# The rounded key and query blocks transposed by a plain fp32r product instead of an fp32 transpose

## The chip, the cores and the metric

The program runs on one core of a Trainium2 chip, in one launch. The metric is the device time of one execution in microseconds; the time given for a kernel is the median of its runs.

## The reference, cut to what matters

One layer of a hybrid decoder on 1024 tokens of width 1024, in float32. Each token is normalised and projected into nine groups of 256 columns; pooling, a short gated convolution, a Conformer convolution and a differential attention work on them; one output projection adds the result to the input, and a SwiGLU block of inner width 2816 follows. The part that the change touches is the attention's scores: four heads, each with two maps of 32 columns.

```python
def diff_attention(q, k, v, q_norm_g, k_norm_g, lam, lam_init, subln_g, rel_bias):
    q = rms_norm(q, q_norm_g)
    k = rms_norm(k, k_norm_g)
    ...
        sc = jnp.einsum('bqhmd,bkhmd->bhmqk', qblk, k).astype(jnp.float32) * scale + bias
        sc = jnp.where(dist >= 0, sc, NEG_INF)
        p = jax.nn.softmax(sc, axis=-1)
        a = p[:, :, 0] - lam * p[:, :, 1]
        return jnp.einsum('bhqk,bkhd->bqhd', a.astype(v.dtype), v)
```

The products have to be nearly as exact as float32.

## The kernel before, in words

Every large product is made of three products in fp32r, a rounded float32 that TensorE takes: an operand is split into a rounded part `hi` and a rounded rest `lo`, and hi·hi, hi·lo and lo·hi are summed in PSUM (`mm3`, L138 to L140; the same three as L604 to L606 where they are handed out one at a time). The tokens stand in eight tiles of 128, worked on in four pairs p of 256 tokens.

The stages in order: norms, input projections and convolutions up to 165 us; then the projections of keys, queries and values by tokens (`proj_tok`, L473, the products `mm` L138 to L140 of 256 columns) up to 246 us; then the attention, 16 units u (`unit`, L657), four heads for each of the four pairs, up to about 405 us; then the second norm and the SwiGLU block to the end.

`stack_T` (L498) prepares keys and queries for the scores. For a token tile of 128 and a group g of two heads it makes the tile `kst` (128 partitions, 4 x 128 columns, type fp32r): ScalarE rounds the values into it (`hi`, L505), VectorE or GpSimd writes the rounded rest (`lo`, L506), each twice, in an order in which one product of 128 rows gives hi·hi + hi·lo + lo·hi + lo·lo. Then TensorE transposes the four 128x128 blocks of `kst` into a PSUM tile (L510), and ScalarE copies them to `KT` or `QT` as fp32r (L513). There are 32 such groups of four transposes: 16 for keys and 4 for queries in the stage of the projections (PSUM tile `t`, 80 transposes), 12 for queries within the attention (PSUM tile `tp`, 48). Before, the block is read as float32 (`bitcast(F)`), and the other operand is `ident`, a 128x128 identity in float32, made by GpSimd at the start.

A unit computes scores (L673, PSUM `sc`), VectorE takes the row minimum of the negated scores (L680, L681), ScalarE the exponential (L684), VectorE joins the two maps (L687, L688, tile `pt`); TensorE transposes `pt` (L699), ScalarE rounds it to `at` (L703), VectorE writes the rest (L704), and TensorE multiplies with the values (L708, PSUM `av`: of 256 columns, and of 128 in the last block of each pair). Other products are handed out between these steps to fill TensorE: parts of the output projection (L604 to L606, `fm`, with `sp` and later `mh`, `ml`), norms (L190), later the first products of the SwiGLU block.

The order of the instructions on each engine is not written by hand. A scheduler sets it when the program is built, by priorities and by its own estimate of how long each instruction takes; the tables at the top (`FQ`, `FL`, `FA`, `FB`, `FC`) say how many filling products are handed out at each place. The hardware then runs each engine's list in that order. So an instruction to which the scheduler gives another length can change the order of others.

Of the kernel before, what the change touches and what calls it, by code (L numbers as in the profile page):

```python
# [11 lines left out]
F = mybir.dt.float32  # L12
R = mybir.dt.float32r
# [6 lines left out]
P = 128  # L20
# [46 lines left out]
def tile_hybrid(ctx, tc, x, norm1_g, w_in, pool_w, pool_scale, sconv_w, conf_w, conf_b, ln_g, ln_b,  # L67
                q_g, k_g, lq1, lk1, lq2, lk2, subln_g, w_out, norm2_g, w_gate, w_up, w_down,
                rel_bias, onehot, maskrow, cntinv, out):
    nc = tc.nc  # L70
    V, A, G, T = nc.vector, nc.scalar, nc.gpsimd, nc.tensor
# [11 lines left out]
    def pool(name, bufs=1, side="left", **kw):  # L83
        return tc.tile_pool(name=name, bufs=bufs, side=side, reuse_waits="tile", **kw)

    const = ctx.enter_context(pool("const"))
# [13 lines left out]
    def ps_mm():  # L100
        return psm.tile([P, 512], F, name="mm", tag="mm")
# [3 lines left out]

    ident = const.tile([P, P], F, name="ident")
    make_identity(nc, ident)
    mhalf = const.tile([P, 16], F, name="mhalf")
    G.memset(mhalf, -0.5)
    G.memset(padl, 0.0)  # L110
# [117 lines left out]
    def chunk_mm(W, ps, h, o, c0, n):  # L228
        for kt in range(8):
            ins = mm3(ps[:, o:o + n], (W[0][:, kt], W[1][:, kt]), (hT[h][0][:, kt, c0:c0 + n], hT[h][1][:, kt, c0:c0 + n]),  # L230
                      kt == 0, kt == 7)
        return ins
# [9 lines left out]
    for p in range(4):  # L242
# [18 lines left out]
        for j in range(2):  # L261
            if p % 2 == 0:
                ps0[j][h] = ps_mm()
            ins = chunk_mm(W0[j], ps0[j][h], h, c0, c0, 256)
# [108 lines left out]
    ps = ps_mm()  # L373
# [84 lines left out]
    for q in range(2):  # L458
        ps = ps_mm()
# [38 lines left out]
    def stack_T(kn, dst, isq, ps_new, nm, g, fill=None, p=None):  # L498
        for i in range(2):
            st = misc.tile([P, 4, 128], R, name="kst", tag="mi") if isq else spp.tile([P, 4, 128], R, name="kst", tag="sp")  # L500
            sv = st.rearrange("p m (a b d) -> p m a b d", a=2, b=2)
            src = kn[:, i, g * P:(g + 1) * P].rearrange("p (m d) -> p m d", d=32).unsqueeze(2).broadcast_to([P, 4, 2, 32])
            hi = sv[:, :, 0, :, :] if isq else sv[:, :, :, 0, :]
            lo = sv[:, :, 1, :, :] if isq else sv[:, :, :, 1, :]
            A.copy(hi, src)  # L505
            (G if isq and X3[2 * PO.index(p) + g] else V).tensor_tensor(lo, src, hi.bitcast(F), op=ALU.subtract)  # L506
            for m in range(0, 4, nm):
                ps = ps_new()
                for a in range(nm):
                    ins = T.transpose(ps[:, a * P:(a + 1) * P], st[:, m + a, :].bitcast(F), ident)  # L510
                if fill:
                    fill(ins)
                A.copy(dst[:, m:m + nm, i * P:(i + 1) * P], ps[:, 0:nm * P].rearrange("p (a b) -> p a b", a=nm))  # L513
# [3 lines left out]
    def prep_q(p, g, ps_new, nm, fill=None):  # L517
        QT[p, g] = qtp.tile([P, 4, 256], R, name="QT", tag="QT")
        stack_T(qn[p], QT[p, g], True, ps_new, nm, g, fill, p)

    def use_k(p, ps):
        ln_pair(p)
        kn = qn[p]
        qk_norm(ps, kn.rearrange("p a b -> p (a b)"))
        for g in range(2):
            stack_T(kn, KT[g][:, :, p * 256:(p + 1) * 256], False, ps_t2, 4, g)
# [657 lines left out]
```

## Time and profile before

| what | us |
|---|---|
| median of 3 runs | 1082.94 (1082.12 to 1084.14) |
| the profiled execution | 1081.06 |
| its span, first to last instruction | 1079.3 |
| PE busy in the span | 1051.2 (97%) |
| DVE busy | 732.8 (68%) |
| ACT busy | 438.9 (41%) |
| POOL busy | 222.5 (21%) |
| granted TensorE clock, mean over the span | 1.000 |

PE is TensorE's products, PEld its weight loads (each product loads its stationary operand first, beside the product before it), DVE is VectorE, ACT ScalarE, POOL GpSimd, SP the queue that issues transfers. A product's duration in a row runs from its start to the end of its modelled pipeline, so neighbours overlap; what a product costs TensorE is the distance between starts. Shares of busy time are averages over stages with different limits.

### The profile page before, as it was taken

To read this page: it belongs to the slowest core of one execution; us is meant where nothing else is said; L and a number is where in the kernel's file an instruction comes from. 1 tells how busy PE (TensorE), PEld (TensorE's weight loads), DVE (VectorE), ACT (ScalarE), POOL (GpSimd) and SP (SyncE) were. 2 spreads that over 40 slices of the span, in tenths; PEclk is the share of its full clock that TensorE was granted. 3 is DMA by queue.
4 is the path that set the end of the run, shared out by engine and by line. 5 is a ranking of instruction groups with operands and counts; after the bars stand their busy time and mean duration, and the time that the engine had idled before them with its cause. 6 is when DMAs were issued, how large, how long until landed. Compare 5 with 4: busy or idle time off the path is not lost.

```text
span 1079.3 us, 13508 instructions
## 1 busy us (share of the span) xinstructions
PE 1051.2 (97%) x5203; PEld 875.7 (81%) x5203; DVE 732.8 (68%) x1127; ACT 438.9 (41%) x710; POOL 222.5 (21%) x202
## 2 busy tenths in 40 slices
PE   7999999998989999899999999999999999999998
PEld 7878879996778876788878888888888888888886
DVE  5599984657899966888677675556656567555541
ACT  5512124545786766432332333333333244333320
POOL 5137114655676653000000000000000000000000
PEclk9999999999999999999999999999999999999999
DMA  8131210111021121014576663233223268766721
GB/s 216 49 98 40 59 39 20 40 40 40 30 71 47 50 81 37 14 54 154 210 280 244 250 208 108 73 112 127 88 79 127 106 228 296 246 195 214 231 101 39
DMA packets 89664, 128.04 MB, mean 119 GB/s; under 512 B 17112, under 2 KB 57600, under 8 KB 87040
## 3 DMA queue, kind: packets, MB, share of 16 engines
q1 hardware_dynamic: 89600, 127.18, 36.0%
q8 instruction: 41, 0.67, 0.3%
q14 instruction: 23, 0.19, 0.1%
HBM read 94.13 MB, written 33.04 MB: 118 GB/s over the span
## 4 chain that ended last, share of the span: by engine, by line
PE 81%; DVE 9%; DMA 5%; ACT 2%; issue 1%; POOL 1%; SPq 0%; ACTq 0%; DVEq 0%; POOLq 0%
PE sb L140 10%; PE sb L138 10%; PE sb L139 10%; PE mm L138 6%; PE mm L139 6%; PE mm L140 6%; PE dx L140 3%; PE dx L138 3%; PE dx L139 3%; PE dy L140 3%; PE dy L138 3%; PE dy L139 3%; DMA wd<-in_w_down_dram 2%; DMA dT<-wd 2%; PE fm L606 1%; PE fm L604 1%
## 5 line engine op out<-in xcount | busy, mean ns | idle before, releaser
L138 PE MATMUL sb<-T,rhi 128*128 128x512 f32 x320 | 125.6, 392 | 0.0
L140 PE MATMUL sb<-T,rlo 128*128 128x512 f32 x320 | 125.5, 393 | 0.0
L139 PE MATMUL sb<-T,rhi 128*128 128x512 f32 x320 | 125.5, 392 | 0.0
L911 DVE TENSOR_TENSOR dq<-ds,dq 128x2048 fp32r<-128x2048 f32 x35 | 80.1, 2291 | 60.3 <-ACT dq L910 60.1
L910 ACT CAST dq<-ds 128x2048 fp32r<-128x2048 f32 x35 | 66.8, 1910 | 105.5 <-PE dy L140 39.6
L134 POOL TENSOR_TENSOR wlo<-st,whi 128x1024 fp32r<-128x1024 f32 (+2 forms) x30 | 73.4, 2449 | 113.0 <-ACT whi L120 101.9
L138 PE MATMUL mm<-hT,whi 128*128 128x512 f32 (+1 forms) x224 | 81.0, 373 | 2.4 <-ACT whi L120 1.9
L139 PE MATMUL mm<-hT,whi 128*128 128x512 f32 (+1 forms) x224 | 82.8, 373 | 0.3 <-DVE hT L200 0.2
L140 PE MATMUL mm<-hT,wlo 128*128 128x512 f32 (+1 forms) x224 | 82.1, 370 | 0.0
L317 DVE SCALAR_TENSOR_TENSOR t<-u,cw,t 128x1023 f32<-128x1023 f32 (+28 forms) x58 | 71.4, 1267 | 0.7
L138 PEld LDWEIGHTS sb<-T,rhi 128*128 128x128 f32 x320 | 60.1, 188 | 13.7 <-DVE tp L1030 0.4
L139 PEld LDWEIGHTS sb<-T,rhi 128*128 128x128 f32 x320 | 60.1, 188 | 13.5
L140 PEld LDWEIGHTS sb<-T,rlo 128*128 128x128 f32 x320 | 60.1, 188 | 13.5
L910 ACT CAST rhi<-st 128x1024 fp32r<-128x1024 f32 x28 | 29.4, 1051 | 85.2 <-PE sb L139 46.5
L140 PE MATMUL dx<-dq 128*128 128x512 f32 x160 | 62.4, 390 | 0.0
L139 PE MATMUL dx<-dq 128*128 128x512 f32 x160 | 62.3, 389 | 0.0
L138 PE MATMUL dx<-dq 128*128 128x512 f32 x160 | 61.9, 390 | 0.0
L684 ACT ACTIVATE pt<-sc,mx 128x128 f32<-128x128 f32 (+7 forms) x64 | 47.6, 747 | 18.2 <-DVE mx L681 18.2
L138 PE MATMUL mm<-whi,hT 128*128 128x256 f32 x192 | 54.8, 288 | 0.0
L139 PE MATMUL mm<-wlo,hT 128*128 128x256 f32 x192 | 54.5, 285 | 0.0
L140 PE MATMUL mm<-whi,hT 128*128 128x256 f32 x192 | 54.4, 284 | 0.0
L120 ACT CAST whi<-st 128x1024 fp32r<-128x1024 f32 x28 | 29.4, 1050 | 58.8 <-PE mm L139 52.8
(342 smaller groups left out, 2683.6 us busy)
## 6 DMA issues: line engine op xcount, KB each, us to landing
ds<-dL SPq DMA_DIRECT2D x35, 512.0 KB, 4.0
wd<-in_w_down_dram SPq DMA_DIRECT2D x10, 1024.0 KB, 5.0
dT<-wd SPq DMA_DIRECT2D x10, 1024.0 KB, 4.0
dL<-afs SPq DMA_DIRECT2D x10, 1024.0 KB, 4.4
ds<-dT SPq DMA_DIRECT2D x20, 512.0 KB, 5.4
st<-in_w_in_dram SPq DMA_DIRECT2D x18, 512.0 KB, 3.7
st<-in_w_gate_dram SPq DMA_DIRECT2D x15, 512.0 KB, 4.0
st<-in_w_up_dram SPq DMA_DIRECT2D x15, 512.0 KB, 3.6
```

Source lines behind the costliest of these rows:

```text
L120: A.copy(dst, src)
L134: G.tensor_tensor(lo[:, nv:], st[:, nv:], hi[:, nv:].bitcast(F), op=ALU.subtract)
L138: T.matmul(ps, lhsT=L[0], rhs=Rr[0], start=first, stop=False, skip_group_check=more)
L139: T.matmul(ps, lhsT=L[0], rhs=Rr[1], start=False, stop=False, skip_group_check=more)
L140: return T.matmul(ps, lhsT=L[1], rhs=Rr[0], start=False, stop=last, skip_group_check=more)
L317: V.scalar_tensor_tensor((z if s == 30 else acc)[:, s:], u[:, :S - s], w[:, 30 - s:31 - s], acc[:, s:], op0=ALU.mult, op1=ALU.add)
L604: yield lambda: T.matmul(ps, lhsT=L[0], rhs=Rr[0], start=first, stop=False)
L606: yield lambda: T.matmul(ps, lhsT=L[1], rhs=Rr[0], start=False, stop=last)
L684: A.activation(pts[m][:, 0:w], sc[:, 0:w], AF.Exp, bias=mx, scale=-1.0, accum_out=lt[:, h, m, i:i + 1])
L910: A.copy(hi, src)
L911: (eng or V).tensor_tensor(lo, src, hi.bitcast(F), op=ALU.subtract)
```

## The change

A second identity, `identr`, of type fp32r is made by a ScalarE copy of `ident`. L510 becomes a plain product: the fp32r block of `kst` is the stationary operand as it is, `identr` the moving one. The values are already rounded, so the product with ones and zeros gives the same numbers. Nothing else in the source changes; lines after L107 stand two lines further down, so L510 is L512 in the changed kernel, L673 is L675, and so on.

```diff
     ident = const.tile([P, P], F, name="ident")
     make_identity(nc, ident)
+    identr = const.tile([P, P], R, name="identr")
+    nc.scalar.copy(identr, ident)
...
-                    ins = T.transpose(ps[:, a * P:(a + 1) * P], st[:, m + a, :].bitcast(F), ident)
+                    ins = T.matmul(ps[:, a * P:(a + 1) * P], lhsT=st[:, m + a, :], rhs=identr, start=True, stop=True)
```

The scheduler sets another order. On TensorE, where the last query projection gives way to the values (about 221 us), `mm` are the projections' products, and before the order is:

```order
L138 MATMUL mm<-whi,hT_101 128x256
L139 MATMUL mm<-wlo,hT_101 128x256
L140 MATMUL mm<-whi,hT_102 128x256
L510 MATMUL t_1868<-ident,kst 128x128 x4
L510 MATMUL t_1877<-ident,kst 128x128 x4
L138 MATMUL mm<-whi,hT_101 128x256
L139 MATMUL mm<-wlo,hT_101 128x256
L140 MATMUL mm<-whi,hT_102 128x256
```

Here the two groups of four transposes follow each other. At the same place the changed kernel has on TensorE:

```order
L141 MATMUL mm<-wlo,hT_103 128x256
L142 MATMUL mm<-whi,hT_104 128x256
L140 MATMUL mm<-whi,hT_103 128x256 x2
L141 MATMUL mm<-wlo,hT_103 128x256
L142 MATMUL mm<-whi,hT_104 128x256
L512 MATMUL t_1870<-identr,kst 128x128 x4
L140 MATMUL mm<-whi,hT_103 128x256
L512 MATMUL t_1879<-identr,kst 128x128 x4
L141 MATMUL mm<-wlo,hT_103 128x256
L142 MATMUL mm<-whi,hT_104 128x256
```

The two groups of key transposes stand some six products later, with one product between them. The other moves in this stage are of one to three products.

On TensorE near the end of the attention (381 us before) `sc` is the last pair of score products of the last unit, `tp<-ident,pt` the transposes of the unit before it. Before:

```order
L673 MATMUL sc<-KT_1365,QT 128x512 x2
L708 MATMUL av<-at,VV_1375 128x256 x2
L751 MATMUL tp<-ident,qn_1379 128x128 x4
L708 MATMUL av<-at,VV_1375 128x256 x2
L699 MATMUL tp<-ident,pt 128x128 x4
L604 MATMUL fm<-whi,mh 128x512
L605 MATMUL fm<-wlo,mh 128x512
L606 MATMUL fm<-whi,ml 128x512
L604 MATMUL fm<-whi,mh 128x512
L605 MATMUL fm<-wlo,mh 128x512
L606 MATMUL fm<-whi,ml 128x512
L699 MATMUL tp<-ident,pt 128x128 x4
```

Here the score products come first. The changed kernel has on TensorE:

```order
L753 MATMUL tp<-ident,qn_1381 128x128 x4
L710 MATMUL av<-at,VV_1377 128x256 x4
L701 MATMUL tp<-ident,pt 128x128 x4
L606 MATMUL fm<-whi,mh 128x512
L607 MATMUL fm<-wlo,mh 128x512
L608 MATMUL fm<-whi,ml 128x512
L606 MATMUL fm<-whi,mh 128x512
L607 MATMUL fm<-wlo,mh 128x512
L608 MATMUL fm<-whi,ml 128x512
L701 MATMUL tp<-ident,pt 128x128 x4
L675 MATMUL sc<-KT_1367,QT 128x512 x2
```

The last score products have moved behind two groups of transposes, the first six `mh`/`ml` products of the output projection and products with the values.

On VectorE over the same time the `pt` of 1024 columns is the last unit's, `fmx` and the ISA rows lead up to it, and `at` belongs to the unit before. Before:

```order
L704 TENSOR_TENSOR at<-tp,at 128x512
L680 TENSOR_REDUCE fmx<-sc 128x1
L686 RECIPROCAL cf<-lt 128x1
L759 SCALAR_TENSOR_TENSOR ml<-tp,subg,mh 128x512
L681 ISA sc,mx<-sc,tb,fmx 128x256
L681 ISA mx 128x1
L704 TENSOR_TENSOR at<-tp,at 128x512
L687 SCALAR_TENSOR_TENSOR cf<-lt,nlam,cf 128x1
L736 SCALAR_TENSOR_TENSOR l_4524<-lt 128x8
L688 SCALAR_TENSOR_TENSOR pt<-pt,cf 128x1024
L704 TENSOR_TENSOR at<-tp,at 128x512
L704 TENSOR_TENSOR at<-tp,at 128x384
```

Here one `at` stands between the last `fmx` and the `pt`, and two stand behind it. The changed kernel has on VectorE:

```order
L706 TENSOR_TENSOR at<-tp,at 128x512
L682 TENSOR_REDUCE fmx<-sc 128x1
L706 TENSOR_TENSOR at<-tp,at 128x512
L683 ISA sc,mx<-sc,tb,fmx 128x256
L683 ISA mx 128x1
L689 SCALAR_TENSOR_TENSOR cf<-lt,nlam,cf 128x1
L738 SCALAR_TENSOR_TENSOR l_4526<-lt 128x8
L690 SCALAR_TENSOR_TENSOR pt<-pt,cf 128x1024
L706 TENSOR_TENSOR at<-tp,at 128x384
```

Now two `at` of 512 stand on either side of the last `fmx`, and only the last `at`, of 384 columns, stands behind the `pt`. On SP the order is unchanged; on ACT the table load and the one new CAST stand first, and some thirty instructions of the attention change places with neighbours.

## Rows read from the trace of the kernel before

**Rows 1.** Stretches: us, busy time and count by engine, clock, DMA

```profile
core 0: us, PE busy (x) PEld busy (x) DVE busy (x) ACT busy (x) POOL busy (x), PEclk, DMA share, GB/s
182.00:246.00 64.00, 64.00 (x549) 64.00 (x548) 34.17 (x62) 31.77 (x63) 39.72 (x31) 1.00 0.11 34
246.00:340.00 94.00, 85.42 (x471) 69.36 (x470) 85.43 (x252) 67.27 (x178) 62.15 (x63) 1.00 0.16 51
340.00:380.00 40.00, 40.00 (x236) 34.45 (x235) 37.26 (x78) 28.62 (x54) 25.97 (x28) 1.00 0.13 41
380.00:470.00 90.00, 82.88 (x412) 65.18 (x411) 68.62 (x130) 48.95 (x87) 23.70 (x20) 1.00 0.15 47
```

**Rows 2.** L510 alone: duration in ns min/median/max, first and last start

```profile
L510 PEld LDWEIGHTS t<-ident,kst x80: 138/140/144, 182.8 to 244.5; 128*128 128x128 f32 x80
L510 PE MATMUL t<-ident,kst x80: 270/273/277, 182.9 to 244.6; 128*128 128x128 f32 x80
...
L510 PE MATMUL tp<-ident,kst x48: 270/273/328, 263.4 to 361.2; 128*128 128x128 f32 x48
```

**Rows 3.** Timeline of PE: start us, duration us, line, tiles, shape, count

```profile
182.80 0.28 PE L140 MATMUL mm<-whi,hT 128*128 128x256 f32 x1
182.92 1.03 PE L510 MATMUL t<-ident,kst 128*128 128x128 f32 x8
183.71 0.36 PE L138 MATMUL mm<-whi,hT 128*128 128x256 f32 x1
183.91 0.27 PE L139 MATMUL mm<-wlo,hT 128*128 128x256 f32 x1
```

**Rows 4.** Timeline of PE around one fp32r product of 128 columns

```profile
289.53 0.22 PE L708 MATMUL av<-at,VV 128*128 128x128 f32 x1
289.59 0.44 PE L605 MATMUL fm<-wlo,sp 128*128 128x512 f32 x1
289.87 0.39 PE L606 MATMUL fm<-whi,sp 128*128 128x512 f32 x1
290.10 0.40 PE L604 MATMUL fm<-whi,sp 128*128 128x512 f32 x1
```

**Rows 5.** Timeline of PEld at the same place: each product's weight load

```profile
289.53 0.19 PEld L605 LDWEIGHTS fm<-wlo,sp 128*128 128x128 f32 x1
289.64 0.19 PEld L606 LDWEIGHTS fm<-whi,sp 128*128 128x128 f32 x1
289.87 0.19 PEld L604 LDWEIGHTS fm<-whi,sp 128*128 128x128 f32 x1
```

**Rows 6.** Groups by shape, 246 to 470 us: count, busy us, mean ns

```profile
L708 PE MATMUL av<-at,VV 128*128 128x128 f32 x32 | 7.1, 222 | 0.0
```

**Rows 7.** Waits of PE, 246 to 470 us: total us, times, longest

```profile
PE av L708 <- DVE at L704: 3.1, 3, 1.3
...
PE tp L699 <- DVE pt L688: 1.9, 4, 0.8
```

**Rows 8.** Timeline of PE and DVE, end of the attention, waits in brackets

```profile
381.12 0.61 PE L673 MATMUL sc<-KT,QT 128*128 128x512 f32 x2
...
382.96 0.50 PE L708 MATMUL av<-at,VV 128*128 128x256 f32 x2 [0.56 <-DVE at L704]
...
390.12 0.50 PE L708 MATMUL av<-at,VV 128*128 128x256 f32 x2 [1.28 <-DVE at L704]
...
392.58 0.62 PE L699 MATMUL tp<-ident,pt 128*128 128x128 f32 x4
...
387.19 2.28 DVE L688 SCALAR_TENSOR_TENSOR pt<-pt,cf 128x1024 f32<-128x1024 f32 x1
```

**Rows 9.** Timeline of ACT and POOL at the start

```profile
0.72 1.28 ACT L170 ACT_TABLE_LOAD   x1 [0.72 <-PEq L1172]
4.53 0.63 ACT L170 ACTIVATE xn<-xt 128x512 f32<-128x512 f32 x1 [2.53 <-DMA xt<-in_x_dram]
...
1.10 0.29 POOL masks.py:199 TENSOR_SCALAR_AFFINE_SELECT ident<-ident 128x128 f32<-128x128 f32 x1
```

## The prediction

> **What bounds the kernel now.** I read the stretches first, then the line of the transposes, then the timeline around one group of them, then the waits. The stretches [rows 1] say where TensorE sets the pace: from 182 to 246 us it is busy for all of the 64.00 us, and from 340 to 380 us for all of 40.00. Around the second it stands still at times: 94.00 - 85.42 = 8.6 us between 246 and 340, and 90.00 - 82.88 = 7.1 us between 380 and 470. The changed line [rows 2] has 80 of its 128 transposes, from 182.8 to 244.5 us, in the stretch without idle time, and 48, from 263.3 to 361.1, in the attention. In the first stretch every nanosecond of the new product counts, in either direction. In the attention VectorE is busy for 85.43 of the 94 us [rows 1] and TensorE waits for it as often as for anything [rows 7]; there a nanosecond counts in part.
>
> **What a transpose costs now.** In the timeline [rows 3] eight transposes start at 182.92, and the second product after them starts at 183.91. The usual step between products of 256 columns is 0.12 (182.80 to 182.92), and one of the two products after the group has that step. So the eight cost 183.91 - 182.92 - 0.12 = 0.87 us, 109 ns each. (The first product behind them starts only 0.03 after the last transpose, but its own successor comes 0.20 after it, so the distance must be read over both.) 128 of them are 14.0 us.
>
> **What the new product costs.** No row shows four such products in succession, but 32 products of the same kind are there: fp32r, a 128x128 stationary block and 128 moving columns, in the multiplication with the values [rows 6]. One row of them lasts 222 ns against 273 of the transpose [rows 2], so its stream through the array is shorter by about 50 ns. That is what "single-pass" promises, and it is not what TensorE pays. In [rows 4] such a product starts at 289.53, the next at 289.59, but that one's successor comes at 289.87, 0.28 later where the step between products of 512 columns is 0.23 (289.87 to 290.10). Over both, the product of 128 columns costs 289.87 - 289.53 - 0.23 = 0.11 us. The reason stands in the weight loads [rows 5]: the load for the next product starts at 289.53 and the one after it at 289.64. A weight load of an fp32r block holds the loading path for 0.11 us; beside a product of 256 or 512 columns that is hidden, beside one of 128 it is not. The old transpose is the opposite case: its load is the shorter one (140 ns in its row [rows 2], 190 in [rows 5]), and its product the longer.
>
> So I take 0.11 us for each new product, that is 110 to 111 ns, against 109. The direct term is 128 x (+1 to +2 ns) = +0.1 to +0.3 us; I take +0.1. The bounds: the least is the step of 0.06 to the next start (289.53 to 289.59), if loads of successive short products could overlap after all: 128 x (60 - 109) = -6.3 us, of which 80 x 49 ns = 3.9 us lie in the stretch without idle time. The most is the step of the next wider shape, 0.12: 128 x 11 = +1.4 us. The nearest row is the same shape itself, so the value is near the middle and not at the lower end.
>
> The Trainium skill, TensorE: Matmul & The Clock Gate, section "LDWEIGHTS", gives a load as the number of columns over 1.2 GHz, which for 128 is 107 ns; the trace agrees with 0.11 between loads [rows 5]. The same page, section "Back-to-back issue gap", measures about 81 ns for each product in a stream of loads and products of 128 columns; by it the sum would be an estimated 128 x (81 - 109 ns) = -3.6 us. No row here has such a stream, and the lone products speak for 0.11.
>
> **The added copy.** ScalarE writes `identr` once. It loads its table from 0.72 to 2.00 and then stands idle until the first input lands at 4.53; `ident` is ready at 1.39 [rows 9]. A copy of 128 columns has 2.5 us of room and needs a fraction of it. Cost 0; if that cover were gone, its own length, which cannot be over the 0.63 of the four times wider ACTIVATE behind it [rows 9].
>
> **What moves in the first stretch.** Transposes move by one to seven products of 0.12 us among products that need none of them. TensorE has no wait here, and its queue stays as long. The keys that come up to 0.8 us later are read by scores only after 246 us. Cost 0.
>
> **What moves in the attention.** This is the larger unknown. From about 300 us the scheduler's order changes, and at the end it changes most. Before, the last score products start at 381.12 and the last `pt` ends at 387.19 + 2.28 = 389.47, a chain of 8.35 us; its first transposes start at 392.58, so it has 3.1 us to spare [rows 8]. In the new order the scores come later and between them and those transposes stand, by my count of the rows, 18 products of 512, 10 of 256, two of 128 and seven transposes: 18 x 0.23 + 10 x 0.12 + 2 x 0.11 + 7 x 0.109 = 6.3 us. So that slack is gone and the chain, if it still took 8.35, would be 2.05 late. But the chain was long because VectorE had other work in its queue; in the new order one `at` fewer stands behind the long `pt`, and the two waits for `at` behind `pt` of 0.56 and 1.28 us [rows 8] have more products in front of them. I expect 2.05 against 0.56 + 1.28 = 1.84, so +0.2, and nothing at the smaller moves, since the same work stands in the same engines. Bounds: no wait left between 380 and 470 us beyond what the norms ask, -2.5 (the 1.84 and some 0.7 of other small ones out of 7.1); or one more wait of 2.05 in the stretch from 340 to 380 that now has none, with both old ones kept, about +4.
>
> **Sum.** +0.1 and 0 and 0 and +0.2 make +0.3 on the profiled execution of 1081.06 us (its span of 1079.3 and 1.8 around it): 1081.4. That execution lies 1.9 below the median of the runs, 1082.94, and I carry the same difference over: 1083.2 us.
>
> **Rivals.**
> 1. The shorter stream shows: successive short products cost 60 ns. For it speaks the duration of 222 against 273, against it the load at 289.64. It gives 3.9 us before 246 us and half of 48 x 49 ns = 2.4 us in the attention, -5.1 us: 1077.9. Chance 0.11.
> 2. Loads and products overlap in part in a row of four or eight, at about 85 ns, half way between 60 and 111: 80 x 24 ns = 1.9 and half of 48 x 24 ns, -2.5 us: 1080.5. The measured stream that the Trainium skill gives (above) lies here. Chance 0.07.
> 3. The later scores decide. The place is the transposes of `pt` in the last two units; the price is 2.05 us each, less the 1.84 that goes, so +2.3, and with the direct term at up to +1.4 some +3: 1085.9. It decides from the point where the chain from scores to `pt` takes more than 6.3 + 1.84 us. For it speaks that VectorE is busy 37.26 of the 40 us from 340 to 380 [rows 1]; against it that the scores were early before. Chance 0.20.
> 4. The new order saves the two waits and adds none, -2.5 us: 1080.5. Chance 0.07.
>
> That the change does nothing at all to the time is the forecast itself: a product with another limit for the same price.
>
> **How the numbers follow.** 0.2% is 2.2 us, about what a measurement of this kernel can tell from no change. The forecast, between -1.5 and +2 us, has 0.55. Faster by over 0.2%: rival 1 with 0.11, most of rivals 2 and 4 with 0.11, together 0.22. Slower: most of rival 3 and the top of the forecast, 0.20. Within: 0.58. The range for 8 in 10 leaves out the lower half of rival 1 and the upper part of rival 3: 1078.3 to 1086.6. The forecast's own range is 1081.4 to 1085.2.
>
> **What would show it.** Right: in the profile after, the products of L512 last about 220 ns, but eight of them still take 0.87 to 0.90 us by the same reading over two successors, with their weight loads 0.11 apart and 190 ns long; the stretch from 182 us ends within 0.4 us of 246. Wrong, by rival 1: starts 0.06 apart throughout and the projections over 3 us earlier. For the order: waits of TensorE for `pt` L690 or `at` L706 after 340 us, against 3.1 and 1.9 us now [rows 7]. My prediction fails at its main step if the eight take under 0.7 us.

## The result and the profile after

| what | us |
|---|---|
| before, median of 6 runs beside it | 1083.1 (1080.13 to 1085.98) |
| after, median of 6 runs | 1088.2 (1087.79 to 1091.12) |
| ratio | 1.0054, 95% interval 1.0033 to 1.0074 |
| the profiled execution after | 1089.98, its span 1088.2 |

The change makes the kernel 5.1 us slower by the two medians. The ratio in the table, from which later sections work, is not their quotient (1.0047); it would make 5.8 us. The forecast was 1083.2, with a range up to 1086.6. The two profiled executions are 8.9 us apart (1081.06 and 1089.98), so some of what follows belongs to one execution and not to the change.

**The new product.** The changed line in the profile after, as [rows 2] (min/median/max in ns):

```profile
L512 PEld LDWEIGHTS t<-identr,kst x80: 187/192/193, 181.6 to 243.6; 128*128 128x128 f32 x80
L512 PE MATMUL t<-identr,kst x80: 218/273/278, 181.7 to 243.7; 128*128 128x128 f32 x80
L512 PE MATMUL tp<-identr,kst x48: 221/276/330, 262.3 to 360.6; 128*128 128x128 f32 x48
```

And the timeline of PE around the first eight, as [rows 3]:

```profile
181.57 0.28 PE L142 MATMUL mm<-whi,hT 128*128 128x256 f32 x1
181.69 1.00 PE L512 MATMUL t<-identr,kst 128*128 128x128 f32 x8
182.53 0.33 PE L140 MATMUL mm<-whi,hT 128*128 128x256 f32 x1
182.70 0.28 PE L141 MATMUL mm<-wlo,hT 128*128 128x256 f32 x1
```

By the same reading as in the prediction, over two successors, the eight cost 182.70 - 181.69 - 0.12 = 0.89 us, 111 ns each, against 0.87 before. The duration in the row is not the 222 ns of the lone product [rows 6]: in a row of them it is 273. I read the difference as the wait for the product's own weight load; the rows do not show it apart. The loads of the eight, in the timeline of PEld, from the first to the one behind them:

```profile
181.57 0.98 PEld L512 LDWEIGHTS t<-identr,kst 128*128 128x128 f32 x8
182.47 0.19 PEld L140 LDWEIGHTS mm<-whi,hT 128*128 128x128 f32 x1
```

(182.47 - 181.57) / 8 = 0.11 us from load to load.

**Where the time went.** The stretches, as [rows 1]:

```profile
182.00:246.00 64.00, 64.00 (x544) 63.91 (x543) 32.44 (x63) 32.46 (x64) 39.56 (x31) 1.00 0.11 34
246.00:340.00 94.00, 84.86 (x465) 68.78 (x464) 85.41 (x252) 66.98 (x178) 61.12 (x63) 1.00 0.16 51
340.00:380.00 40.00, 39.20 (x226) 33.21 (x225) 34.40 (x72) 26.53 (x52) 23.58 (x28) 1.00 0.12 41
380.00:470.00 90.00, 81.13 (x404) 63.11 (x403) 67.81 (x129) 49.95 (x89) 24.49 (x20) 1.00 0.16 47
```

The stretch from 340 to 380 us has lost its full PE (40.00 to 39.20), and VectorE does 2.9 us less there (37.26 to 34.40). To place the loss I compared the start of the same product of TensorE in both traces; the numbers are after minus before, in us, at the product that stood at the given time before:

| trace | 25 | 244 | 340 | 440 | 570 | 620 |
|---|---|---|---|---|---|---|
| after | -1.2 | -1.0 | -0.2 | +3.8 | +3.0 | +8.9 |

The start is 1.2 us earlier in this execution. The 80 products before 246 us cost +0.2. Between 293 and 306 us +0.8 is lost, then between 340 and 440 +4.0. At the product that stood at 380 the shift is already +2.4, up from -0.5 at 366. But from 360 to 415 many products have changed places, so that the shift of one product holds its own move too. Counted instead by the work that TensorE had started (each product at its usual step of 0.23, 0.12 or 0.11 us for 512, 256 or 128 columns, so an estimate), the shift goes from -0.1 at 366 to +2.4 at 380 and +3.2 at 382, back to +1.8 at 392, where the two old waits lay, and up again to +4.0 at 430. From 540 to 570 us 0.8 is regained, and behind 574 us comes another +5.9. The waits of PE from 246 to 470 us, as [rows 7], with two more rows of before ahead of those of after:

```profile
PE sc L673 <- ACT pt L684: 1.5, 2, 0.8
PE fm L604 <- DVE x L774: 0.8, 2, 0.4
```

```profile
PE tp L701 <- DVE pt L690: 3.0, 6, 0.8
PE av L710 <- DVE at L706: 2.3, 4, 1.3
PE sc L675 <- ACT pt L686: 2.1, 4, 0.8
PE fm L606 <- DVE x L776: 1.5, 2, 0.8
PE fm L606 <- ACT tm L773: 0.8, 2, 0.5
PE tp L192 <- DVE h2lo L202: 0.8, 1, 0.8
PE tp L192 <- DVE at L706: 0.7, 1, 0.7
```

The wait for `pt` has grown from 1.9 to 3.0; the one for `at` behind `pt` has shrunk from 3.1 to 2.3, as forecast; and a wait of score products for `sc` buffers that ScalarE still reads, one for `x` and one for `h2lo` have grown or come. PE before had the two waits of [rows 8], at 383 and 390 us; the timeline of PE now has five small ones from 379 to 387 us:

```profile
378.46 0.40 PE L606 MATMUL fm<-whi,sp 128*128 128x512 f32 x1
379.25 0.68 PE L675 MATMUL sc<-KT,QT 128*128 128x512 f32 x2 [0.39 <-ACT pt L686]
380.73 0.73 PE L675 MATMUL sc<-KT,QT 128*128 128x512 f32 x2 [0.24 <-ACT pt L686]
381.94 0.55 PE L701 MATMUL tp<-ident,pt 128*128 128x128 f32 x3 [0.47 <-DVE pt L690]
...
384.93 0.51 PE L710 MATMUL av<-at,VV 128*128 128x256 f32 x2 [0.61 <-DVE at L706]
...
386.20 0.50 PE L606 MATMUL fm<-whi,mh 128*128 128x512 f32 x1 [0.33 <-ACT mh L760]
```

The five make 2.04 us in the brackets, the two made 1.84. But a bracket is not the whole price of a wait: it begins only where the product before it ends. From the first row to the second the starts are 0.79 us apart, where the step between products of 512 columns is 0.23 [rows 4]; that is 0.56 lost, with 0.39 in the bracket. By this reading many small waits cost more than few long ones of the same sum. PE stands idle for 5.2 us from 340 to 440 us before and for 7.8 from 340 to 443.75 after; these 2.5 us are only a part of the +4.0.

At the place that the prediction had worked out, the last pair of score products and the last `pt`, nothing is lost to `pt`:

```profile
388.38 0.71 PE L675 MATMUL sc<-KT,QT 128*128 128x512 f32 x2
...
393.84 1.29 DVE L690 SCALAR_TENSOR_TENSOR pt<-pt,cf 128x1024 f32<-128x1024 f32 x1
```

The chain takes 393.84 + 1.29 - 388.38 = 6.75 us instead of 8.35, and its first transposes start at 396.55 without a wait.

**Behind 574 us.** A transfer of a block of `w_down` lands late here, VectorE waits for it, and PE behind VectorE; the granted clock falls to half. The DVE row, the PE row, and the stretch from 582 us:

```profile
581.86 0.69 DVE L1049 TENSOR_TENSOR wd<-wd 128x512 f32<-128x512 f32 x1 [6.72 <-DMA wd<-in_w_down_dram]
```

```profile
583.21 0.80 PE L140 MATMUL sb<-T,rhi 128*128 128x512 f32 x1 [3.05 <-DVE tp L1032]
```

```profile
582.00:590.00 8.00, 6.79 (x17) 5.41 (x18) 7.79 (x12) 0.09 (x1) 0.00 (x0) 0.57 0.43 152
```

Some 3 us of wait and some 3 us at half clock make the +5.9. The prediction had said nothing of this place.

### The profile page after: what moved, and what is told of

It reads as the page before. It is cut to its first block, busy times and chain, and to the rows that moved or that the text cites. A ratio compares the mean times of both kernels' runs of the same rounds, so it can differ in the third digit from the quotient of the medians.

```text
span 1088.2 us, 13506 instructions
## 1 busy us (share of the span) xinstructions
PE 1054.9 (97%) x5203; PEld 876.9 (81%) x5203; DVE 732.2 (67%) x1127; ACT 438.8 (40%) x711; POOL 221.1 (20%) x202
## 4 chain that ended last, share of the span: by engine, by line
PE 78%; DVE 9%; DMA 7%; ACT 2%; POOL 1%; issue 1%; SPq 0%; ACTq 0%; DVEq 0%; POOLq 0%
PE sb L140 10%; PE sb L141 9%; PE sb L142 9%; PE mm L142 6%; PE mm L141 6%; PE mm L140 6%; PE dx L140 3%; PE dx L142 3%; PE dx L141 3%; DMA wd<-in_w_down_dram 3%; DMA dT<-wd 3%; PE dy L140 3%; PE dy L141 3%; PE dy L142 2%; PE fm L606 1%; PE fm L607 1%
```

## The experiments

Theory A: the order that the scheduler made costs the time, at the end of the attention above all. Rival B: the product or its weight load. Rival C: the copy. Rival D: the late transfer and the clock come at random.

**Order and product taken apart.** The kernel is built as before (or as after); when the order stands, the logged products are exchanged in place, with their waits and signals, for the other kind:

```diff
                     ins = T.transpose(ps[:, a * P:(a + 1) * P], st[:, m + a, :].bitcast(F), ident)
+                    SW.append((ins.ins, st[:, m + a, :], identr, isq))
...
+    swap(nc, R)        # behind the schedule: fp32r operands, no transpose mode
     r = _run(nc, [arrays], core_ids=[0])
```

> The order that the scheduler made for the transposes, on every engine, with the 128 transposes then exchanged for the fp32r products with the fp32r identity, in place; ScalarE's copy of the identity is there. Theory A (the order alone costs the time, mainly at 294 to 306, 367 to 391 and 415 to 428 us): as before, ratio 1.000, within 1.5 us, and the trace runs within 0.5 us of the one before up to the end of the attention. Rival B (the product or its weight load costs the time): +4 to +5 us, most of it already seen by 428 us. Rival C (the copy or the start): a shift in the first 30 us, +1 us or more. Rival D (the late load of w_down at 573 us and the half clock behind it come at random): the attention as before, and whether the late load shows is a matter of chance.

Measured: 1083.88 (12 runs) against 1083.47 (17), ratio 0.9995 (0.998 to 1.0011). With the old order the product costs nothing that can be measured. In the table of shifts: -1.12 at 25 us, -0.98 at 244, -0.18 at 440; 0.9 of this comes at 244 to 260, where its clock is halved for a while (0.98 in the mean from 246 to 340 us), so the expected 0.5 us was missed there by the clock; from 260 to 440 us the shift stays between 0.0 and -0.2. Its waits of PE from 246 to 470 us are those of before:

```profile
PE av L711 <- DVE at L707: 3.0, 3, 1.3
...
PE tp L702 <- DVE pt L691: 1.7, 4, 0.8
PE sc L676 <- ACT pt L687: 1.5, 2, 0.8
```

The counterpart takes the order of after and exchanges the new products for fp32 transposes, `swap(nc, F, True)`.

> The counterpart: the order that the scheduler made for the new product, on every engine, with fp32 transposes put back in place. Theory A: as the changed kernel, ratio 1.004 to 1.006, +4 to +5 us through the attention (366 to 391 and 415 to 428 us). Rival B: as before, within 1.5 us. Rival D: if the half clock behind the w_down load belongs to this order it shows again, a further +6 us in its profile; if it is chance it may not.

Measured: 1088.18, ratio 1.0051 (1.0031 to 1.0071), the whole of the change's loss without one new product. Shifts: 0.0 at 244 us, +0.8 at 340, +5.3 at 440. Theory A stands, as far as order against product goes; B and C fall.

**The price by itself.** The same exchange, each product issued twice in a row (`swap(nc, times=2)` and `swap(nc, R, times=2)`).

> The order before, each of the 128 fp32 transposes issued twice into the same place. By the price of 109 ns read from the timeline: 80 x 109 = 8.7 us before 246 us, where TensorE never waits, and in the attention between 0 and 48 x 109 = 5.2 us; in all 8.7 to 13.9 us, +10 to +13 us likely. If the duration in the row (273 ns) were the price: 22 us before 246 us.

> The order before with the fp32r products, each issued twice. If one costs 110 ns (bound by its weight load): +8.8 us before 246 us against one issue, in all as with the doubled transposes, within 1.5 us of them. If it streams at 60 ns: 4.8 us before 246 us, and in all some 5 us less than the doubled transposes. At about 85 ns: 6.8 us.

Measured: 1093.89, ratio 1.0107 (1.0083 to 1.0131), and 1096.8, ratio 1.0128 (1.0109 to 1.0147). The price is read in the stage without idle time, from the first of the 80 (or 160) to the second successor of the last. The last row needed, in the timelines of PE of before, of the exchanged kernel, and of the two doubled ones:

```profile
244.88 0.28 PE L138 MATMUL mm<-whi,hT 128*128 128x256 f32 x1
```

```profile
181.77 0.44 PE L512 MATMUL t<-identr,kst 128*128 128x128 f32 x3
...
243.91 0.28 PE L140 MATMUL mm<-whi,hT 128*128 128x256 f32 x1
```

```profile
183.67 1.91 PE L512 MATMUL t<-ident,kst 128*128 128x128 f32 x16
...
254.28 0.28 PE L140 MATMUL mm<-whi,hT 128*128 128x256 f32 x1
```

```profile
183.19 1.90 PE L512 MATMUL t<-identr,kst 128*128 128x128 f32 x16
...
254.26 0.28 PE L140 MATMUL mm<-whi,hT 128*128 128x256 f32 x1
```

Before, from 182.92 [rows 3]: 61.96 us; doubled 70.61; so 8.65 / 80 = 108 ns for a transpose. New: 62.14, doubled 71.07; 8.93 / 80 = 112 ns. Exchanged once, 62.14 - 61.96 = +0.18 us for 80. The prediction had 109 and 110 to 111. The expectation that the doubled kernels lie within 1.5 us of each other missed: 2.9 apart in the medians. In their traces, 4.6 apart, the stage makes 0.3 of it; the new one's clock is halved at 263 us (1.1), and its `w_down` transfer is late (2.0).

**Which part of the order.** Only the eight transposes of one query group are written as the new product, then all but these, then four of these eight:

```diff
-                    ins = T.matmul(ps[:, a * P:(a + 1) * P], lhsT=st[:, m + a, :], rhs=identr, start=True, stop=True)
+                    ins = T.matmul(ps[:, a * P:(a + 1) * P], lhsT=st[:, m + a, :], rhs=identr, start=True, stop=True) if fill is not None and (p, g) == (3, 1) else \
+                        T.transpose(ps[:, a * P:(a + 1) * P], st[:, m + a, :].bitcast(F), ident)
```

> Only 8 of the 128 transposes, those of the second query group of the last pair, are written as fp32r products; the scheduler gives the end of the attention the order of the changed kernel, all before 340 us the old one. Theory A (the order at the end costs): +3.5 to +4.5 us, +2.8 us between 366 and 380 us and +1.7 between 403 and 415 as in the changed kernel, nothing at 293 to 306 us; ratio 1.003 to 1.005. Rival B (the products cost): 8 of them, +0.1 us at most.

> The other 120 transposes are fp32r products, those 8 stay fp32 transposes; the scheduler then keeps the old order from about 310 us on. Theory A: +0.2 us for the products and the one +0.8 between 293 and 306 us, in all +1.0, between 0 and +1.5 us; the end of the attention no later than that. Rival B: +4 to +5 us as in the changed kernel.

> Only 4 of the 128 transposes are fp32r products: the first token tile of the last query group. The scheduler gives the end of the attention the same order as with all 8 of that group. Theory A: as with the 8, +3 to +4.5 us. If the price hung on the number of products, a thirty-second part of the change's +5: nothing.

Measured: eight alone 1087.26, ratio 1.0038 (1.0025 to 1.0052); the other 120 1084.04, ratio 1.0012 (0.9999 to 1.0025), not clear of no change; four alone 1088.68, ratio 1.0047 (1.003 to 1.0063). Shifts from 340 to 440 us: +2.9, +0.1 and +4.4; from 293 to 306 us: 0, +0.8 and 0. So four products, at the same price as the transposes they stand for, cost over 4 us, by the order that the scheduler then makes of the end of the attention: on PE the first move stands at 360 us and the last at 415.

**Late scores or misplaced fill.** In the new order the score products of the last two units stand 4 to 22 products later. Five changes to the table of fill (`FQ`) of the changed kernel move them or leave them:

```diff
-FQ[123], FQ[124] = 6, 2; FQ[161] = 12
+FQ[123], FQ[124] = 0, 0; FQ[161] = 20        # fewer_fills_11
-FQ[127], FQ[128], FQ[129] = 5, 4, 2; FQ[161] = 12
+FQ[127], FQ[128], FQ[129] = 0, 0, 0; FQ[161] = 23        # fewer_fills_12
-FQ[172], FQ[173] = 13, 10; FQ[145], FQ[147] = 0, 0
+FQ[172], FQ[173] = 9, 6; FQ[145], FQ[147] = 4, 4        # more_fills_13
-FQ[172], FQ[173] = 13, 10; FQ[166], FQ[167] = 0, 0
+FQ[172], FQ[173] = 9, 6; FQ[166], FQ[167] = 4, 4        # fills_at_scores_15
-FQ[157], FQ[158] = 14, 6; FQ[141], FQ[142] = 0, 0
+FQ[157], FQ[158] = 10, 2; FQ[141], FQ[142] = 4, 4        # more_fills_12
```

> The changed kernel, with the 8 filling products of unit 11's last two places (FQ 123 and 124) handed out later, at FQ 161. By the order the score products of the last two units stand within some 13 products of their old ranks on either side instead of 4 to 22 later. Theory A with late scores as the cause: between a half and all of the +2.8 us at 366 to 380 comes back, ratio 1.000 to 1.003. If the scores' place isn't the cause: as the changed kernel, 1.005. If TensorE lacks work in unit 12 instead: a new wait there, up to +2 us more.

> The changed kernel, with 11 of the filling products of unit 12 (FQ 127 to 129) handed out later, at FQ 161. The scores of the last two units then stand some 5 products ahead of their old ranks (from 13 ahead to 12 behind). Late scores as the cause: the +2.8 us at 366 to 380 comes back, in part or whole, ratio 0.999 to 1.003. If they aren't: as the changed kernel. The other side: TensorE waits for scores' buffers or pt at 345 to 365 us, up to +3 us, because unit 12 has less to fill it.

> The changed kernel with 8 filling products handed out earlier: 4 from FQ 172 and 4 from FQ 173 (unit 15) moved to FQ 145 and 147 (unit 13). If what the new order lost is fill at 366 to 400 us, some of the waits there go and the work behind the attention gets shorter: 1 to 3 us back, ratio 1.002 to 1.004. If late scores are the cause: the scores stand 9 to 22 products later than before the change, no better, ratio 1.005 or more.

> The changed kernel with 8 filling products of unit 15 handed out behind its first two score pairs (FQ 166 and 167) instead of behind its transposes (FQ 172 and 173). The scores keep the changed kernel's ranks. If fill between the last scores and their transposes is what is short: 0.5 to 1.5 us back, ratio 1.003 to 1.005. If not: as the changed kernel, 1.005.

> The changed kernel with 8 filling products of unit 14 (4 from FQ 157, 4 from FQ 158) moved forward to unit 13's first places (FQ 141 and 142). By the order the scores of units 14 and 15 stand up to 22 products later than before the change, the last pair only 2. If the last scores' place decides: up to 2 us back. If the fills' place decides, 1 to 3 us back; if neither, 1.005.

Measured, in this order: 1.0099 (1.0083 to 1.0115), 1.0116 (1.0096 to 1.0137), 1.0122 (1.0102 to 1.0142), 1.0106 (1.0085 to 1.0128), and 1.0029 (1.0015 to 1.0043). Both kernels with fewer fills, whose scores come earlier, are 5 to 8 us slower than the changed one; but they also took fill out of units 11 and 12, so late scores are not cleared by them. Nor is it simply lack of fill: two kernels with fill further ahead are as slow as these. What they lose beyond the changed kernel from 340 us on lies at the products that stood between 403 and 421 us before, where the fill no longer reaches and a transpose stands behind the norm's tiles. Waits of PE from 362 to 450 us with the fill at the scores of unit 15:

```profile
PE fm L606 <- DVE x L776: 2.9, 4, 1.9
PE tp L722 <- DVE h2lo L202: 2.7, 1, 2.7
PE tp L192 <- DVE h2lo L202: 1.5, 1, 1.5
```

A part of it is the clock: behind this wait of 2.7 us the granted clock is 0.54 in the mean from 425 to 432 us, and in the other kernel, behind the same wait, 0.57 from 423 to 431 us.

Only the last kernel, with eight fills moved from unit 14 to unit 13, gives back about half of the loss (1085.1), though its interval overlaps that of the change. Its last score pair stands 2 products late instead of 22, so this run can't tell the place of the fills from the place of the last scores. It doesn't beat the kernel before. The same instructions, in six orders, take between 1085 and 1097 us.

**Casts in ScalarE's queue.** In the changed kernel the cast of the last part of `w_out` waits on ScalarE for its transfer, the next exponential stands right behind it, and VectorE waits for that. Timelines of ACT and of DVE:

```profile
377.05 1.05 ACT L122 CAST whi<-st 128x1024 fp32r<-128x1024 f32 x1 [1.93 <-DMA st<-in_w_out_dram]
378.00 1.11 ACT L686 ACTIVATE pt<-sc,mx 128x1024 f32<-128x1024 f32 x1
```

```profile
379.23 1.33 DVE L689 SCALAR_TENSOR_TENSOR cf<-lt,nlam,cf 128x1 f32<-128x1 f32 x1 [1.45 <-ACT pt L686]
```

Before, that cast stands behind one more exponential. Moving it to another engine tests it:

```diff
-WOE = [0, 0, 1, 0, 1, 0, 0, 0]
+WOE = [0, 0, 1, 0, 1, 0, 2, 2]        # then 1, 1; then 2, 0; then 2, 0 in the kernel before
```

> The changed kernel, but the two rounding casts of the last part of w_out (WOE 6 and 7) go to GpSimd; on ScalarE they stand ahead of an exponential at 377 and 384 us and the first waits 1.93 us for its transfer. The score products keep the changed kernel's ranks except for the last pair. If these casts in ScalarE's queue are what holds the softmax chain back: 1 to 3 us back, ratio 1.002 to 1.004. If late scores or the fill cause it: 1.005, unchanged. Against it: the cast is slower on GpSimd, and the output projection's products wait for it, up to 4 us more.

> The same with both casts on VectorE. If ScalarE's queue is the cause: part of 1 to 3 us back, less than with GpSimd, since VectorE carries the chain too. If late scores or the fill cause it: 1.005 or somewhat more.

> The same with only the first of the two casts on GpSimd, the one that waits 1.93 us at 377 us. ScalarE's queue as the cause: 1 to 2 us back. Otherwise 1.005.

> The kernel before, fp32 transposes, with the first cast on GpSimd. There it waits for nothing and no exponential stands late behind it: no change, or up to +2 us by the slower cast and the new order behind it.

Measured: 1.0082 (1.0052 to 1.0111), 1.0042 (1.0025 to 1.006), 1.0054 (1.0033 to 1.0074), and in the kernel before 1.0001 (0.9983 to 1.0018). The wait it was meant to remove goes: that of the score products for ScalarE at 362 to 396 us falls from 0.6 to 0.2 with both on GpSimd:

```profile
PE sc L675 <- ACT pt L686: 0.2, 1, 0.2
```

The time doesn't come back: other waits grow from 362 to 396 us, for `at` from 1.0 to 2.0 with both on GpSimd and to 2.4 with both on VectorE, for `pt` from 0.5 to 1.0 with VectorE and 1.5 with one cast on GpSimd. The slower cast that I had expected on GpSimd isn't there, 1.04 us against 1.05 on ScalarE. With VectorE the interval reaches from half of the change's loss to all of it. So these edits show no gain from moving the casts, but they don't clear the casts of a share of the loss.

The traces name a candidate that no edit tested, the transfer for which the first cast waits. Between 355 and 445 us the chain of work that ended last runs through this transfer in all four kernels with the whole new end of the order, and not in the kernel before, the old order with the new product, or the kernel with fills moved from unit 14 to unit 13. With the eight alone and after the change it took, from issue to landing:

```profile
372.92 3.51 DMA st<-in_w_out_dram
```

```profile
372.54 4.43 DMA st<-in_w_out_dram
```

With four alone it took 4.72, with the new order and the old product 5.14. The losses from 340 to 440 us follow in the same sequence: 2.9, 4.0, 4.4 and 4.5. Before, it took 3.5. So some 1 to 1.6 us of the loss go with a slower landing in these executions, and 2.9 are left where it landed as fast as before. Four traces are no test, and what makes the landing slower was not tried.

**The late transfer.** It isn't tied to the order. VectorE's wait for the same block is 3.49 us before, and where it is over 5 us PE waits too. It is short with the new end of the order in one kernel (the eight alone) and long with the old end in another (the new products twice). The rows are of before and of these two:

```profile
575.38 0.69 DVE L1047 TENSOR_TENSOR wd<-wd 128x512 f32<-128x512 f32 x1 [3.49 <-DMA wd<-in_w_down_dram]
```

```profile
579.10 0.69 DVE L1050 TENSOR_TENSOR wd<-wd 128x512 f32<-128x512 f32 x1 [3.63 <-DMA wd<-in_w_down_dram]
```

```profile
591.57 0.69 DVE L1050 TENSOR_TENSOR wd<-wd 128x512 f32<-128x512 f32 x1 [5.54 <-DMA wd<-in_w_down_dram]
```

What makes it late was not tried.

## Why the prediction was wrong

- What bounds the kernel: right. TensorE is busy for all of the stretch before 246 us, and there a nanosecond of the product counts in full.
- Price of the new product: right. 111 ns by the timeline, 112 by doubling, against 108 before; the sum over the 80 is +0.2 us, where +0.1 was taken, and +0.3 at most, for all 128. Rivals 1 and 2 fall. The Trainium skill (TensorE: Matmul & The Clock Gate, "LDWEIGHTS") gives a load as its columns over 1.2 GHz, an estimated 107 ns for 128; the trace has 0.11 us. By its section "Back-to-back issue gap" the products would cost about 81 ns each; the doubled kernels show 112.
- That the new product's row would read about 220 ns: wrong. It reads 273 in a group and near 220 at the least, which I read as the wait for the product's own load. The price read over two successors was not touched by it.
- The added copy: right, cost 0. With it and the new product in the old order the ratio is 0.9995.
- The moves in the first stretch: right, within +0.2 us together with the products.
- **What moves in the attention: this step failed.** I put +0.2 there, with +4 as the upper bound, from one place at its end and a balance of one lost and two saved waits. The order alone costs some +5: +0.8 at 293 to 306 us, where I put nothing, and +4.0 from 340 to 440. By the count of work +2.6 of this lie ahead of the place that I worked out (381 to 392 us before), about -0.6 within it and +2.2 behind it. At that place the chain shrank from 8.35 to 6.75 us and PE did not wait for `pt` at all, so the 2.05 of my sum did not come. The wait for `at` fell from 3.1 to 2.3, but the smaller moves, which I put at nothing, gave waits to `pt`, `sc`, `x`, `tm` and `h2lo`. "The same work stands in the same engines" was the wrong ground for that: the work of PE to 440 us is the same, and 2.5 us more idle time stand in it. I also took the idle time in the brackets for the price of a wait; by the starts a wait of 0.39 us cost 0.56.
- Rival 3, that later scores decide, came nearest in size (+3, 1085.9) and in sign, with 0.20. Its mechanism is not shown: the transposes of the last `pt` did not wait, and the two kernels with earlier scores were slower, with less fill.
- What stays open: which of the moves at 362 to 415 us is the first cause. The loss is spread over five or six waits of 0.3 to 1 us, and each edit that took one away put others in its place. The transfer of the last part of `w_out` is a candidate; issuing it earlier was not tried.
- A slip in the numbers, which decides nothing: -1.5 to +2 us around 1082.94 is 1081.4 to 1084.9, where the prediction has 1085.2.
- The parts: eight products alone +4.1 us (0.0038 of 1083), the other 120 +1.3, together 5.4 against 5.8 (0.0054) for the whole; the 1.3 alone are not clear of zero. The 8.9 us between the two profiled executions are -1.2 at the start, +5.0 to 440 us, -0.8 from 540 to 570, and +5.9 by the late transfer and the halved clock.

## What to carry to other kernels

An fp32r product with a stationary block of 128 columns and 128 moving ones cost here what lies between two weight loads (0.11 us), so its shorter row (222 against 273 ns when alone) bought nothing against the transpose at 108: price a product by starts, not by its row. Where a scheduler sets the order from its own estimates, an edit of equal cost on the chip is still an edit of the whole order: fix the order and exchange the instruction, then compare, before giving the time to the instruction. A table of fill that was fitted to one order belongs to that order; with another it can cost more than the edit could have given.

## What the runs showed of the hardware

The granted clock falls to half (1.2 of 2.4 GHz) for short times in nearly every execution: the mean over the span is 0.989 to 0.999 in nearly all, and 1.000 in the profiled one before. In the traces it falls where TensorE stands still or has just done so, as around the 3.05 us of wait at 582 us above, where wait and half clock together cost 5.9 us, about twice the wait. Not every wait does it: with the new order and the old product the wait at the same place was 2.3 us, and the clock was 1.00 from 570 to 600 us. Nor do the same waits always do it: before the change and in the old order with the new product TensorE had the same three waits of 0.7 to 0.8 us from 248 to 254 us, and the granted clock from 246 to 262 us was 1.00 in the one and 0.89 in the other. The profile before, free of such falls, lay 2 us under its own median. An alignment of two single traces can take such a stretch for an effect of the change.
